# Three pieces of side work moved in a two-layer diffusion backbone on one core: modulation sums spread over a down projection, row scaling moved into a projection, output weights split later

## The chip, the cores and the metric

The kernel runs on one core of a Trainium2 chip. The metric is the device time in microseconds of one execution; the median of three runs is taken. The core's engines are TensorE (PE, with its weight loads PEld), VectorE (DVE), ScalarE (ACT), GpSimd (POOL) and SyncE (SP). All matrix work is done in float32 as three matmuls on split operands: every operand is written as a rounded high part (a cast on ACT) and a rest (a subtraction on DVE or POOL), and high×high, high×low and low×high are summed.

## The reference

Two layers over 1024 latent tokens and 256 context tokens of width 1024. Every layer computes a modulation of six rows from a condition vector, a mixer (attention), and a feed-forward block with a convolution along the sequence; each sub-layer ends in `LayerNorm(alpha*x + gate*f)`.

```python
m_lat = split(silu(c) @ ada_w[l] + ada_b[l], 6)          # shift, scale, gate, twice
h = x * (1 + m[1]) + m[0]
y = mixer(h)                                             # layer 0: global + neighbourhood; layer 1: window, sink
x = layer_norm(alpha * x + m[2] * y, ln_g[l, 0], ln_b[l, 0])
u = modulate(x, m[3], m[4]) @ w_up                       # 1024 -> 2 x 2816, three-tap convolution
f = (silu(g) * a) @ w_down                               # 2816 -> 1024
x = layer_norm(alpha * x + m[5] * f, ln_g[l, 1], ln_b[l, 1])
```

The modulation of a layer depends on nothing but `c` and `ada_w`, so it can be computed at any time before its use.

## The kernel before, in words

The kernel is a sequence of stages: the modulation of layer 0 and the first projections (to about 390 us of the trace), the two attentions of layer 0 (to about 807), their output projection, the feed-forward of the context (925 to 1130), that of the latent tokens (up 1130 to 1578, down 1578 to 1884), layer 1's projections (`l1_project`, 1884 to about 2025), its attention (`attn_c`, to 2279), its output projection (`l1_out`, to about 2384) and its feed-forward. Within most stages a scheduler orders the instructions of each engine; in the feed-forward (`ffn2`) and the attention the order is the order of the code.

**The down phase of `ffn2`.** The output of 1024 tokens by 1024 columns is made in two halves of 512 columns. A half has NP = 22 steps, one for each 128 rows of the hidden width; a step has eight token tiles of three matmuls (`mm`, lines 339 to 341), into eight PSUM banks. `load` (L1526 for weights of two steps, L1530 for the hidden rows `g`) fetches what a later step needs, six steps ahead (`last`), and splits it: ACT casts and DVE subtracts (L1536 and L1537 for g, L99 and L100 for weights). Steps 2 to 9 load a row tile z, steps 4 to 11 scale one (L1725, L1726). After the last step of the first half each bank is multiplied by the gate on DVE (`tt`, L1744), which frees the bank for the second half. The generator `side` computes layer 1's modulation ahead: `ada_ahead` has 24 pieces here; a piece loads 256 KB (L228, tile `araw`, two buffers) and, one piece later, DVE multiplies and adds twice (L235, L237). Every fourth piece's sum goes to DRAM (L241). SP issues all these loads in order, and one whose buffer is not free holds those behind it.

**`l1_project`.** `proj_tok` loads and splits weights (`load_in`, L112; cast L99, subtraction L100 on POOL), multiplies tile by tile, and hands each to `ev_q` (rotary on DVE, L381 and L391, and POOL, L395; then transposed, L416, and stored) or `ev_kv`. The order is: queries of the first 512 columns, context rows transposed (`build_hT`: four transposes L322, four evictions L328 into one `hst` buffer, then h and its rest, L333 and L334), keys and values, queries of the second 512 columns. The weights pass through `raw`, a pool of two buffers. `ada_reduce` sums the modulation's partial sums over partitions (load L271 into `accr`, cast L255, two small matmuls L259 and L260), two yields after each query tile.

**`attn_c` and `l1_out`.** `side` is a table of what runs beside which group of the attention: ten splits of output weights (`out_weight`, cast L1086, subtraction L1087), then sixteen row scalings (`scale_row`, L1892 and L1893 on POOL) of the rows x2 that `l1_out` reads. `l1_out` loads and splits the last three rows of weights before its first tile; for later tiles yh and yl are made of a loaded yr (L1141, L1142).

Of the kernel before, what the change touches and what calls it, by code (L numbers as in the profile page):

```python
# [17 lines left out]
KT = 8  # L18
# [18 lines left out]
class Kern:  # L37
# [229 lines left out]
    def ada_reduce(self, tp, bank, l, v, parts):  # L267
        for part in parts:
            for o in range(0, D, 512):
                acc = self.t(tp, [128, 512], "accr", bufs=2)  # L270
# [818 lines left out]

    def out_weight(self, w_out, k, h, r):  # L1090
# [23 lines left out]
    def out_project(self, w_out, yT, order, xsrc, gate_of, finish, st, wx, pp,  # L1114
# [6 lines left out]
        for k in range(5, KT):  # L1121
            r = self.t(self.raw, [128, 2, 512], "raw")
            nc.sync.dma_start(r, w_out[k * 128 : (k + 1) * 128].rearrange(
                "p (h n) -> p h n", n=512))
            for h in range(2):
                ws[k, h] = self.split_out(self.t(wx, [128, 2, 512], "w", R), r[:, h])
# [46 lines left out]
    def l0_out(self, h2l, h2c, pu):  # L1173
        nc, io, d = self.nc, self.io, self.d
        with ExitStack() as es:
# [5 lines left out]
            gates = {}  # L1181

# [303 lines left out]
    def ffn2(self, l, B, hps, T, dT, xsrc, gate_row, view, begin, finish, norm, jobs=(),  # L1486
# [209 lines left out]
        with ExitStack() as es, self.tc.manual_schedule(engines=every):  # L1696
# [20 lines left out]
            with ExitStack() as e2:  # L1717
# [13 lines left out]
                for i in range(NP):  # L1731
# [16 lines left out]
                    if 4 <= i < 4 + NLAT:  # L1748
                        scale(i - 4)
                    elif i > 4:  # L1750
                        for _ in range(3):
                            next(side, None)
                for _ in side:
                    pass
                bank = [self.t(pd, [128, 512], f"d{t}") for t in range(NLAT)]
                for i in range(NP, NP + 4):
                    load(i + last)
                    for t in range(NLAT):
                        mm(i, t, bank[t])
                    for t in (2 * (i - NP), 2 * (i - NP) + 1):  # L1760
                        add(0, t, tts[t])
            for i in range(NP + 4, 2 * NP - last):
# [22 lines left out]
    def l1_project(self, H, abc):  # L1785
        nc, io, d = self.nc, self.io, self.d
        with ExitStack() as es:
# [19 lines left out]

            def ev_kv(t, ps):
# [8 lines left out]
            def ev_q(h0):  # L1817
                def ev(t, ps):
                    q = self.t(st, [128, 512], "q", bufs=3)
                    self.rope(st, ps, 8, rp[:, t, 0:HD], rp[:, t, HD:], q)  # L1820
                    for _ in range(2):
                        next(sums, None)
                    return lambda: self.put_T(
# [14 lines left out]
            for t in range(2):  # L1838
                xc = self.t(st, [128, D], "xc", bufs=1)
# [27 lines left out]
    def attn_c(self):  # L1867
        nc, d, io = self.nc, self.d, self.io
        self.mix = (4, 10)
        with self.eC as es:  # L1870
# [8 lines left out]
            xp = es.enter_context(self.pool("cx"))  # L1879
            gb = [self.t(xp, [128, D], f"gb{i}") for i in range(2)]  # L1880
            self.bcast(gb[0], io["ln_g"][0, 1])
            self.bcast(gb[1], io["ln_b"][0, 1])

# [3 lines left out]
            def scale_row(t, h):  # L1887
                x = row()
                s = slice(h * 512, (h + 1) * 512)
                dr = d["x2"][t * 128 : (t + 1) * 128, s]  # L1890
                nc.sync.dma_start(x, dr)
                nc.gpsimd.tensor_mul(x, x, gb[0][:, s])  # L1892
                nc.gpsimd.tensor_add(x, x, gb[1][:, s])  # L1893
                nc.gpsimd.dma_start(dr, x)

            side = {}
            for i in range(10):
# [325 lines left out]
```

## Time and profile before

| | us |
|---|---|
| median of three runs (lowest, highest) | 3084.83 (3080.67, 3086.35) |
| profiled execution | 3084.81 |
| its span, first to last instruction | 3083.0 |
| PE busy | 2846.8 (92%) |
| DVE busy | 2087.5 (68%) |
| ACT busy | 1369.9 (44%) |
| POOL busy | 798.3 (26%) |
| mean granted clock of TensorE | 0.966 |

Busy time is an average over stages. A group of instructions has a line, an engine, an operation, its tiles (out<-in), a count, busy time and mean duration, then the idle time before it and what ended that. A row of a timeline has its start, its duration, and in brackets the idle time before it and what ended it. A row of SP is the issue of a DMA, not its transfer. A row of the windows has the length, then busy time and count for PE, PEld, DVE, ACT and POOL, the granted clock, the share of the DMA engines and GB/s.

### The profile page before, as it was taken

What the parts mean: (1) busy time and instruction counts of PE and PEld (TensorE: products, weight loads), DVE (VectorE), ACT (ScalarE), POOL (GpSimd) and SP (SyncE); (2) the same over time, 40 slices, a digit from 0 to 9 for tenths busy, and PEclk for the clock granted to TensorE, in tenths of its full rate; (3) what the DMA queues carried; (4) which work ended last, traced back from release to release, by engine and by line L of the source; (5) the groups of instructions that cost most, each with busy time, mean ns of one, the idle gap of its engine ahead of it and who ended that gap; (6) DMA issues with size and microseconds to landing.
All of it is one profiled execution on the core that took longest, in us unless ns stands there. A gap on an engine that the chain in (4) does not pass through costs nothing.

```text
span 3083.0 us, 44764 instructions
## 1 busy us (share of the span) xinstructions
PE 2846.8 (92%) x16564; PEld 2293.9 (74%) x16564; DVE 2087.5 (68%) x3705; ACT 1369.9 (44%) x2579; POOL 798.3 (26%) x961
## 2 busy tenths in 40 slices
PE   6889989899997989999999498989998899999998
PEld 2767767777787977888888476866677688888887
DVE  3687766666587877888876535356667677777755
ACT  2222155567435655444552234256653444545330
POOL 3651033354464420000000003336855000000001
PEclk7999999999998999999999799999999999999999
DMA  7366731023556544333365524443344322223742
GB/s 246 100 178 211 217 121 32 17 100 110 168 157 212 192 139 122 108 107 110 113 246 170 176 82 152 129 140 98 122 137 144 119 77 79 82 82 132 286 135 83
DMA packets 330039, 418.57 MB, mean 136 GB/s; under 512 B 22826, under 2 KB 245530, under 8 KB 328282
## 3 DMA queue, kind: packets, MB, share of 16 engines
q1 hardware_dynamic: 314124, 367.87, 38.1%
q0 software_dynamic: 12800, 46.14, 4.1%
q8 instruction: 130, 2.13, 0.3%
q10 hardware_dynamic: 2896, 1.70, 0.2%
q14 instruction: 89, 0.73, 0.1%
HBM read 318.85 MB, written 96.80 MB: 135 GB/s over the span
## 4 chain that ended last, share of the span: by engine, by line
PE 47%; DMA 4%; DVE 4%; POOL 4%; ACT 2%; issue 2%; SPq 0%; ACTq 0%; POOLq 0%; DVEq 0%
PE q L1546 8%; PE x L1546 8%; PE y L1546 8%; PE v L1546 4%; PE d L339 4%; PE d L341 4%; PE d L340 4%; PE mm L341 1%; PE mm L339 1%; PE mm L340 1%; POOL P L657 1%; PE pv L738 1%; DMA raw<-in_down_dram 1%; PE o L341 1%; PE T L729 1%
## 5 line engine op out<-in xcount | busy, mean ns | idle before, releaser
L657 POOL TENSOR_SCALAR P<-P,rin 128x640 f32<-128x640 f32 (+3 forms) x288 | 248.9, 869 | 311.1 <-DVE rin L656 281.3
L1448 DVE TENSOR_TENSOR w<-raw,w 128x512 fp32r<-128x512 f32 x308 | 208.8, 691 | 163.2 <-ACT w L1446 163.0
L339 PE MATMUL d<-w,w 128*128 128x512 f32 x704 | 276.1, 392 | 39.1 <-DVE tt L1744 39.1
L99 ACT CAST w<-raw 128x512 fp32r<-128x512 f32 x276 | 162.5, 620 | 256.7 <-PE d L341 126.2
L340 PE MATMUL d<-w,w 128*128 128x512 f32 x704 | 275.4, 391 | 0.0
L341 PE MATMUL d<-w,w 128*128 128x512 f32 x704 | 275.2, 391 | 0.0
L100 POOL TENSOR_TENSOR w<-raw,w 128x512 fp32r<-128x512 f32 x100 | 149.2, 1513 | 405.1 <-ACT w L99 403.7
L1593 POOL DMA_DIRECT2D g<-cv x44 | 23.5, 534 | 873.8 <-DVE cv L1592 873.8
L633 PE MATMUL S<-k,q 64*128 64x256 f32 (+2 forms) x1824 | 194.3, 339 | 15.7 <-DVE nm L1942 6.3
L100 DVE TENSOR_TENSOR w<-raw,w 128x512 fp32r<-128x512 f32 x176 | 135.4, 807 | 98.9 <-ACT w L99 98.8
L654 ACT ACTIVATE P<-P,nm 128x641 f32<-128x641 f32 (+4 forms) x208 | 161.6, 778 | 89.9 <-DVE nm L1942 33.8
L1446 ACT CAST w<-raw 128x512 fp32r<-128x512 f32 x308 | 182.5, 621 | 12.7 <-DVE raw L1453 11.4
L339 PEld LDWEIGHTS d<-w,w 128*128 128x128 f32 x704 | 133.2, 189 | 67.0 <-ACT w L99 39.5
L633 PEld LDWEIGHTS S<-k,q 64*128 64x128 f32 x1824 | 137.3, 189 | 51.8 <-issue 17.9
L644 ACT COPY PT<-T 128x512 f32<-128x512 f32 (+1 forms) x250 | 134.2, 566 | 84.1 <-PE T L764 79.8
L1537 DVE TENSOR_TENSOR w<-raw,w 128x512 fp32r<-128x512 f32 x176 | 112.5, 686 | 65.4 <-ACT w L1536 65.3
L340 PEld LDWEIGHTS d<-w,w 128*128 128x128 f32 x704 | 133.1, 189 | 27.7
L341 PEld LDWEIGHTS d<-w,w 128*128 128x128 f32 x704 | 133.0, 189 | 27.7
L778 PE MATMUL pv<-PT,v 128*64 128x128 f32 x2016 | 134.2, 281 | 14.6 <-ACT PT L644 12.0
L764 PE MATMUL T<-ident,P 128*128 128x128 f32 x1008 | 137.9, 284 | 9.5 <-POOL P L657 5.4
L1536 ACT CAST w<-raw 128x512 fp32r<-128x512 f32 x176 | 98.9, 618 | 106.1 <-PE d L341 56.4
L205 DVE SCALAR_TENSOR_TENSOR acc<-araw,cs,acc 128x512 f32<-128x512 f32 x168 | 132.0, 838 | 12.9 <-DMA araw<-in_ada_w_dram 12.4
(327 smaller groups left out, 7730.8 us busy)
## 6 DMA issues: line engine op xcount, KB each, us to landing
raw<-in_up_dram SPq DMA_DIRECT2D x132, 512.0 KB
raw<-g SPq DMA_DIRECT2D x88, 512.0 KB
raw<-in_down_dram SPq DMA_DIRECT2D x66, 512.0 KB
araw<-in_ada_w_dram SPq DMA_DIRECT2D x48, 512.0 KB
g<-cv POOLq DMA_DIRECT2D x44, 512.0 KB, 3.0
araw<-in_ada_w_dram SPq DMA_DIRECT2D x64, 256.0 KB
raw<-in_w_in_dram SPq DMA_DIRECT2D x28, 512.0 KB
wt<-in_ada_w_dram SPq DMA_DIRECT2D x16, 512.0 KB
```

Of the source, the lines that this page charges most:

```text
L99: nc.scalar.copy(hi, s)
L100: (lo_eng or nc.vector).tensor_sub(lo, s, f32(hi))
L339: nc.tensor.matmul(ps, lh, rh, start=first, stop=False)
L340: nc.tensor.matmul(ps, lh, rl, start=False, stop=False)
L341: nc.tensor.matmul(ps, ll, rh, start=False, stop=last)
L633: self.nc.tensor.matmul(outs[a], q[r, x, qs], k[r, y, ks], start=(i == 0), stop=(i == 2))
L654: nc.scalar.activation(P[:, :m], P[:, :m], AF.Exp, bias=negm, scale=-1.0, accum_out=den)
L657: nc.gpsimd.tensor_scalar(P[:, :n], P[:, :n], rin, 1.0, ALU.mult, ALU.mult)
L764: nc.tensor.transpose(ps[:, s * 128 : (s + 1) * 128], P[a][:, cols[i + x] : cols[i + x] + 128], self.ident,)
L1446: nc.scalar.copy(half(i, 0), src[i])
L1448: nc.vector.tensor_sub(half(i, 1), src[i], f32(half(i, 0)))
L1546: nc.tensor.matmul(ps, w[:, a, s], r[b][:, k], start=first and k + i == 0, stop=k == 3 and i == 2, skip_group_check=True,)
```

## The change

In the down phase a modulation piece is issued in each step from 1 to 21, also in those that scale a row, and one in each of the first four steps of the second half; before, three were issued in each of the steps 12 to 21. In `l1_project` each query tile scales one half row tile of x2 on DVE (`scale_rows`: load on SP, multiply, add, store on POOL's queue; two `xs` buffers), and the context rows use `raw` buffers; `accr` has one buffer where it had two. In `attn_c` the row scaling and its two broadcasts are gone, and four splits of output weights are left of ten; side[4] loads the rest. `l1_out` splits them before its first tile, into ten buffers where it had six.

```diff
@@ ada_reduce
-                acc = self.t(tp, [128, 512], "accr", bufs=2)
+                acc = self.t(tp, [128, 512], "accr", bufs=1)
@@ output weights
+    def load_out(self, pool, w_out, k):
+        r = self.t(pool, [128, 2, 512], "w" if pool is self.ring else "raw")
+        self.nc.sync.dma_start(
+            r, w_out[k * 128 : (k + 1) * 128].rearrange("p (h n) -> p h n", n=512)
+        )
+        return r
+
+    def out_rows(self, w_out, k0):
+        n = KT - 4
+        self.wrows = {
+            k: self.load_out(self.raw if k < n else self.ring, w_out, k)
+            for k in list(range(n, KT)) + list(range(k0, n))
+        }
@@ out_project
-        for k in range(5, KT):
-            r = self.t(self.raw, [128, 2, 512], "raw")
-            nc.sync.dma_start(r, w_out[k * 128 : (k + 1) * 128].rearrange(
-                "p (h n) -> p h n", n=512))
+        for k in range(KT):
+            if (k, 0) in ws:
+                continue
+            if k in self.wrows:
+                r = self.wrows[k]
+            else:
+                r = self.load_out(self.raw, w_out, k)
             for h in range(2):
-                ws[k, h] = self.split_out(self.t(wx, [128, 2, 512], "w", R), r[:, h])
+                w = self.t(wx if k < KT - 1 or not self.wrows else self.ring, [128, 2, 512], "w", R)
+                ws[k, h] = self.split_out(w, r[:, h])
@@ ffn2, down phase
                     if 4 <= i < 4 + NLAT:
                         scale(i - 4)
-                    elif i > 4:
-                        for _ in range(3):
-                            next(side, None)
-                for _ in side:
-                    pass
+                    if i:
+                        next(side, None)
                 bank = [self.t(pd, [128, 512], f"d{t}") for t in range(NLAT)]
                 for i in range(NP, NP + 4):
                     load(i + last)
                     for t in range(NLAT):
                         mm(i, t, bank[t])
+                    next(side, None)
                     for t in (2 * (i - NP), 2 * (i - NP) + 1):
                         add(0, t, tts[t])
+                for _ in side:
+                    pass
@@ l1_project
+            gb = {}
+
+            def scale_rows(i):
+                h, t = divmod(i, NLAT)
+                s = slice(h * 512, (h + 1) * 512)
+                if t == 0:
+                    for n in ("ln_g", "ln_b"):
+                        gb[n] = self.t(st, [128, 512], n)
+                        self.bcast(gb[n], io[n][0, 1, s])
+                x = self.t(st, [128, 512], "xs", bufs=2)
+                dr = d["x2"][t * 128 : (t + 1) * 128, s]
+                nc.sync.dma_start(x, dr)
+                nc.vector.tensor_mul(x, x, gb["ln_g"])
+                nc.vector.tensor_add(x, x, gb["ln_b"])
+                nc.gpsimd.dma_start(dr, x)
...
                     for _ in range(2):
                         next(sums, None)
+                    scale_rows(t + (NLAT if h0 else 0))
...
-                xc = self.t(st, [128, D], "xc", bufs=1)
+                xc = self.t(self.raw, [128, D], "raw")
@@ attn_c
-            for i in range(10):
-                side[2 + i] = lambda i=i: self.out_weight(io["w_out1"], i // 2, i % 2, row())
-            for i in range(16):
-                side[12 + i] = lambda i=i: scale_row(i // 2, i % 2)
+            side = {4: lambda: self.out_rows(io["w_out1"], 2)}
+            for i in range(4):
+                side[12 + 3 * i] = lambda i=i: self.out_weight(
+                    io["w_out1"], i // 2, i % 2, row()
+                )
@@ l1_out
-            wx = es.enter_context(self.pool("wx1", bufs=6))
+            wx = es.enter_context(self.pool("wx1", bufs=10))
```

On SP, in the down phase of layer 0 from the end of the scaling steps on, there stands before (`raw<-g` is the load of a step's hidden rows, `raw<-in_down_dram` that of two steps' weights, `araw` that of a modulation piece):

```order
L1530 DMA raw_16125<-g_96 128x1024
L228 DMA araw_16158<-in_ada_w_dram 128x2x256
L228 DMA araw_16160<-in_ada_w_dram 128x2x256
L228 DMA araw_16164<-in_ada_w_dram 128x2x256
L1530 DMA raw_16168<-g_96 128x1024
L228 DMA araw_16200<-in_ada_w_dram 128x2x256
L228 DMA araw_16205<-in_ada_w_dram 128x2x256
L228 DMA araw_16209<-in_ada_w_dram 128x2x256
```

And of the changed kernel, on the same queue at about the same steps (its line numbers are some 21 higher):

```order
L1551 DMA raw_16172<-g_96 128x1024
L228 DMA araw_16204<-in_ada_w_dram 128x2x256
L1551 DMA raw_16208<-g_96 128x1024
L228 DMA araw_16241<-in_ada_w_dram 128x2x256
L1547 DMA raw_16245<-in_down_dram 128x2x512
L1551 DMA raw_16253<-g_96 128x1024
L228 DMA araw_16285<-in_ada_w_dram 128x2x256
```

Between two loads of hidden rows stands one piece where three stood.

On TensorE, at the passage from the first query projection to keys and values in `l1_project`, there stands before (`tr<-ident,q` and `tr<-ident,xc` are transposes of a query tile and of context rows, `mm` 128x256 a matmul of the key and value projection):

```order
L416 MATMUL tr_18124<-ident_58,q_17997 128x128 x4
L416 MATMUL tr_18134<-ident_58,q_18051 128x128 x4
L339 MATMUL mm_18222<-w_18208,h1lh_17206 128x256
L340 MATMUL mm_18222<-w_18208,h1lh_17206 128x256
L341 MATMUL mm_18222<-w_18208,h1ll_17207 128x256
```

And of the changed kernel, on the same engine at the same place (the context rows are now named `raw`):

```order
L416 MATMUL tr_18168<-ident_58,q_18026 128x128 x4
L416 MATMUL tr_18178<-ident_58,q_18085 128x128 x4
L416 MATMUL tr_18188<-ident_58,q_18144 128x128 x4
L322 MATMUL tr_18200<-ident_58,raw_18198 128x128 x4
L322 MATMUL tr_18212<-ident_58,raw_18198 128x128 x4
L129 MATMUL small_18681<-ident_58,rt_18676 128x32
L322 MATMUL tr_18226<-ident_58,raw_18224 128x128 x4
L322 MATMUL tr_18238<-ident_58,raw_18224 128x128 x4
L339 MATMUL mm_18266<-w_18252,h1lh_17206 128x256
```

All transposes of the queries and of the context rows, and a small transpose of modulation rows, now stand ahead of the first matmul of keys and values. On SP the load of that matmul's weights stands behind stores of the transposed queries:

```order
L419 DMA qC_22_90<-qst_18173 128x4x128
L419 DMA qC_22_90<-qst_18183 128x4x128 x2
L112 DMA raw_18250<-in_w_in_dram 128x4x256
L265 DMA ada_88<-abr_18159 1x512
L419 DMA qC_22_90<-qst_18193 128x4x128 x2
L112 DMA raw_18258<-in_w_in_dram 128x4x256
```

Before, the same loads (`raw_18206` and `raw_18214`) stood among the stores of x2 at the end of the down phase.

More of the change, by code (lines that the diff above doesn't have):

```diff
@@ L1181, in l0_out @@
             gates = {}
+            self.wrows = {}
             def gate_of(t):
@@ L1878, in attn_c @@
             po = es.enter_context(self.pool("cO", bufs=1, space=PSUM))
[L1879 to L1882, printed above, removed]
             def row():
                 return self.t(Pp, [128, 641], "P")[:, :512]
[L1887 to L1896, printed above, removed]
-            for i in range(10):
-                side[2 + i] = lambda i=i: self.out_weight(io["w_out1"], i // 2, i % 2, row())
-            for i in range(16):
-                side[12 + i] = lambda i=i: scale_row(i // 2, i % 2)
+            side = {4: lambda: self.out_rows(io["w_out1"], 2)}
[3 more added lines that the diff above has]
+                )
             side[28] = lambda: self.out_y(d["yT1"], 0, [row(), row()])
```

## The prediction

> **What bounds the kernel now.** I read the page, then the waits of TensorE, then the windows and the timelines of the places that the diff touches. The page's first part:
>
> ```profile
> PE 2846.8 (92%) x16564; PEld 2293.9 (74%) x16564; DVE 2087.5 (68%) x3705; ACT 1369.9 (44%) x2579; POOL 798.3 (26%) x961
> ```
>
> TensorE is busy in 92% of the span, so 3083.0 − 2846.8 = 236 us is all that a change of order can recover. The longest of its waits (engine, tile, line, who it waited for; total, times, longest), and the rows of TensorE round it:
>
> ```profile
> PE d L339 <- DVE tt L1744: 39.1, 1, 39.1
> ```
>
> ```profile
> 1578.39 0.39 PE L339 MATMUL d<-w,w 128*128 128x512 f32 x1
> ...
> 1697.88 0.39 PE L341 MATMUL d<-w,w 128*128 128x512 f32 x1
> 1737.39 0.76 PE L339 MATMUL d<-w,w 128*128 128x512 f32 x1 [39.12 <-DVE tt L1744]
> ```
>
> These are the two halves of layer 0's down phase. The first half ran from 1578.39 to 1698.1 without a pause: 22 steps in 119.7 us, 5.44 us a step. Then TensorE stood 39.1 us, because its banks are free only when DVE has multiplied them (tt), and DVE was behind. The timeline of DVE shows by how much:
>
> ```profile
> 1645.19 1.22 DVE L1726 TENSOR_TENSOR z<-z,gb 128x1024 f32<-128x1024 f32 x1
> ...
> 1647.54 1.28 DVE L1537 TENSOR_TENSOR w<-raw,w 128x512 fp32r<-128x512 f32 x2
> ...
> 1709.39 2.04 DVE L237 SCALAR_TENSOR_TENSOR acc<-araw,cs,acc 128x256 f32<-128x256 f32 x4
> 1713.15 1.00 DVE L237 SCALAR_TENSOR_TENSOR acc<-araw,cs,acc 128x256 f32<-128x256 f32 x2 [1.72 <-DMA araw<-in_ada_w_dram]
> 1717.00 1.29 DVE L1537 TENSOR_TENSOR w<-raw,w 128x512 fp32r<-128x512 f32 x2 [2.84 <-ACT w L1536]
> ...
> 1735.35 1.29 DVE L1537 TENSOR_TENSOR w<-raw,w 128x512 fp32r<-128x512 f32 x2 [5.25 <-ACT w L1536]
> 1736.56 1.88 DVE L1744 TENSOR_TENSOR tt<-d,gate 128x512 f32<-128x512 f32 x3
> ```
>
> L1537 splits the g rows of one step. From the split at 1647.54 (step 12) to that at 1735.35 (step 21) nine steps took 87.8 us, 9.8 us each, and DVE idled in them. SP's timeline says why:
>
> ```profile
> 1628.35 21.66 SPq L228 DMA_DIRECT2D araw<-in_ada_w_dram  x3
> ...
> 1701.55 10.27 SPq L228 DMA_DIRECT2D araw<-in_ada_w_dram  x3
> 1711.88 0.46 SPq L1530 DMA_DIRECT2D raw<-g  x1
> ```
>
> Three modulation loads go out at a time, two buffers hold them, so the third waits for DVE, and the g load that DVE needs next stands behind it. Layer 1's down phase has the same steps without modulation, and there DVE's split ends just ahead of tt, with no wait of TensorE:
>
> ```profile
> 2947.71 2.50 DVE L1537 TENSOR_TENSOR w<-raw,w 128x512 fp32r<-128x512 f32 x4 [4.75 <-ACT w L1536]
> 2950.12 4.87 DVE L1744 TENSOR_TENSOR tt<-d,gate 128x512 f32<-128x512 f32 x8
> ```
>
> **Part 1, modulation one piece a step.** The work is the same 24 pieces. Each is two operations of 128x256; four of L237 took 2.04 us at 1709.39, so a piece is 1.0 us. Before step 12 eleven pieces are new: DVE ends step 11 at 1646.4 + 11.0 = 1657.4 at most, say 1659 with some waits for loads that are now more. TensorE needs the rows of step 17, which step 11 splits, at 1578.4 + 17 × 5.44 = 1671, so it isn't starved on the way. From there a step asks of DVE a g split of 1.3, half a weight split (0.65) and a piece (1.0), 2.9 us. SP couples them: the g load of a step now waits only for the piece of the step before last. From its issue at 1711.88 to the end of the split at 1718.3 it took 6.4 us; with a piece behind it that is 7.4 us. If two steps share such a round trip, a step is 3.7 us; if each pays a whole one, 7.4. I take 4.75, nearer the first, since one load may stay under way. DVE then reaches tt at 1659 + 9 × 4.75 + 2 = 1704, against TensorE's 1698.1: **a gap of about 5 us is left, −34** (0 at 3.7; at 7.4, 1659 + 67 + 2 = 1728, 30 left). The second half takes four more pieces; its rows are six steps ahead by then, so they cost nothing; without that lead they would cost 4.
>
> The gap has a tail, seen in windows (length, busy time of PE, PEld, DVE, ACT, POOL, granted clock, DMA share, GB/s):
>
> ```profile
> 1660.00:1698.00 38.00, 38.00 (x169) 31.36 (x167) 16.88 (x33) 6.86 (x12) 0.00 (x0) 1.00 0.51 166
> 1698.00:1737.00 39.00, 0.27 (x2) 0.00 (x0) 16.23 (x31) 7.45 (x13) 0.00 (x0) 0.55 0.53 173
> 1737.00:1745.00 8.00, 7.61 (x23) 6.06 (x24) 6.55 (x12) 1.67 (x3) 0.00 (x0) 0.65 0.64 255
> ```
>
> 23 matmuls took 7.61 us where the pace of the first row (38.00/169 = 0.225) asks 5.2: 2.4 us lost at a clock of 0.65. A short pause has a smaller tail. After the one of 6.33 us at 1884:
>
> ```profile
> 1884.27 1.97 PE L322 MATMUL d<-ident,z 128*128 128x128 f32 x8 [6.33 <-ACT z L2059]
> ...
> 1886.46 0.63 PE L340 MATMUL mm<-w,h1lh 128*128 128x512 f32 x1
> ...
> 1889.02 0.56 PE L340 MATMUL mm<-w,h1lh 128*128 128x512 f32 x1
> ```
>
> six matmuls from 1886.46 to 1889.02 went at 0.427, 1.2 us lost. I count half of the 2.4 as gained: **−1.2** (0 to −2.4). The Trainium skill ("TensorE: Matmul & The Clock Gate", What's actually happening) says that one idle window of some 3.4 us halves the clock, however long the pause was beyond that; by it a gap of 5 us keeps the whole tail, and the sum would be 1.2 us later. The row at 1884 lies between.
>
> **Part 2, ctx rows in the weights' buffers.** Both raw buffers now hold xc until its transposes, so the k/v weights load behind them. Now, the k/v splits and TensorE's two short waits at this place, with the chain's load of a weight:
>
> ```profile
> 1934.09 1.59 POOL L395 TENSOR_TENSOR q<-rp,rp 128x512 f32<-128x512 f32 x1 [4.80 <-PE mm L341]
> 1935.64 5.05 POOL L100 TENSOR_TENSOR w<-raw,w 128x512 fp32r<-128x512 f32 x4
> 1940.66 1.27 POOL L395 TENSOR_TENSOR q<-rp,rp 128x512 f32<-128x512 f32 x1
> ...
> 1948.33 1.28 POOL L334 TENSOR_TENSOR h1cl<-hst,h1ch 128x512 fp32r<-128x512 f32 x1 [0.36 <-DVE h1ch L333]
> ```
>
> ```profile
> 1941.99 0.66 PE L416 MATMUL tr<-ident,q 128*128 128x128 f32 x4 [0.72 <-POOL q L395]
> ...
> 1947.39 1.12 PE L322 MATMUL tr<-ident,xc 128*128 128x128 f32 x4 [2.18 <-ACT hst L328]
> ```
>
> ```profile
> 1940.72 4.04 DMA raw<-in_w_in_dram
> ```
>
> Count from the end of the q projection. The third q tile is transposed about 3.5 us later (rope, then L395), xc's first tile by 5.5. Its buffer is free then; the load takes 4.04, to 9.6. The cast on ACT now stands behind three evictions of xc, each held by the one hst buffer through a 1.28 us POOL subtraction, to about 12.5; POOL subtracts that eviction (1.28) and the weight (5.05/4 = 1.26), so full matmuls start at 15. The second half's weights are split by 20, while the first half's matmuls of four tiles fill TensorE. Idle is 15 less 4 of transposes, 11, where now 0.72 + 2.18 = 2.9 are: +8, and a clock tail of 1.2 to 2.4, +2: **+10**. Lower bound +3 (one load and cast barely uncovered, 4.04 + 0.62 + 1.26 − 2.9), upper +18 (the two loads and the evictions in series).
>
> **Part 3, row scaling in the q projections.** 32 DVE operations of 128x512, at 0.65 each (1.29/2, L1537), are 21 us over 16 tiles, 1.3 a tile where TensorE needs 8 × 3 × 0.23 = 5.5; hidden. The loads wait for stores two pieces back, and the modulation sums' loads queue behind those on SP, the more so with one accr buffer; the chain to TensorE's small matmuls has about one tile of slack. I take **+1** (0 to +8 if it stalls a little at each tile). A rule speaks against it: the Trainium skill ("GPSIMD Engine Reference", Specifications) says that GpSimd shares its memory port with DVE instructions that read two operands from SBUF, as these do; L395's 1.59 and 1.27 above, one operation with and without company, fit it. By it the last L395 may be 1.3 us later, and the sum 1.3 us higher, at the boundary only.
>
> **Part 4, what leaves the attention.**
>
> ```profile
> L1893 POOL TENSOR_TENSOR P<-P,gb 128x512 f32<-128x512 f32 x16 | 20.5, 1279 | 0.2
> L1892 POOL TENSOR_TENSOR P<-P,gb 128x512 f32<-128x512 f32 x16 | 20.4, 1278 | 2.3 <-DMA P<-x 2.3
> ```
>
> ```profile
> 2050.00:2110.00 60.00, 55.45 (x484) 38.54 (x480) 42.88 (x116) 43.38 (x102) 28.83 (x63) 1.00 0.28 85
> 2110.00:2230.00 120.00, 112.58 (x982) 75.98 (x980) 79.62 (x216) 81.39 (x187) 100.29 (x165) 1.00 0.37 115
> ...
> 2245.00:2260.00 15.00, 15.00 (x138) 10.54 (x136) 10.96 (x34) 12.21 (x30) 9.95 (x19) 1.00 0.06 19
> ```
>
> POOL loses 40.9 us, and 6 of 10 weight splits go. TensorE idled 4.6 us in the split stretch and 7.4 in the scaling stretch, and 0 where no side work ran: at most −12, and −2 of the start's two broadcasts. Most of the idle time in the attention is put down to ACT's copies, which the change does not touch:
>
> ```profile
> PE pv L738 <- ACT PT L644: 12.8, 23, 1.8
> ```
>
> I take half: **−6** (0 to −14).
>
> **Part 5, the first tile of the output projection.** Ten splits follow each other:
>
> ```profile
> L1086 ACT CAST w<-P 128x512 fp32r<-128x512 f32 x20 | 12.2, 621 | 9.1 <-DMA P<-in_w_out_dram 9.0
> L1087 DVE TENSOR_TENSOR w<-P,w 128x512 fp32r<-128x512 f32 x20 | 15.1, 770 | 9.8 <-ACT w L1086 9.8
> ```
>
> Each feeds three matmuls (0.69 us); four splits are ready ahead (2.7 us), so ACT at 0.62 keeps up and DVE at 0.65 to 0.77 loses at most 10 × 0.08. The second tile's yh cast then stands behind them and six up-weight casts: +3. Those casts and their DVE work no longer stand at the stage's end: −3. **0** (−3 to +4).
>
> **Sum** on the profiled execution (3084.81, span 3083.0 and 1.8 around it; the median is 3084.83): −34 − 1.2 + 10 + 1 − 6 + 0 = −30.2, **3054.6 us**.
>
> **Rivals.**
> - *The gap goes wholly and the attention recovers its idle time*: gap 0 and its tail (−41.5), kv +5, attention −12: 3036. For it: layer 1's tt; against: ACT named in the attention. 0.15.
> - *SP's coupling stays*: a whole round trip each step, 30 us left (−9), the rest as above (+5): 3081. For it: the 5.25 us wait before the last split; against: the third load, which made the wait, is gone. 0.1.
> - *Slower*: pieces in the scaling steps make DVE late from the start. If a step still costs what it did with three pieces, 9.8, in most of 21 steps (8.7 on the mean), the half takes 183 us where TensorE needs 119.7: 63 of waits instead of 39.1, +24, with +5 of the rest: 3114. It decides at (119.7 + 34)/21 = 7.3 us a step. Against: DVE's own work in a scaling step is 2.4 + 2.9 = 5.3. 0.05.
> - *Neither gap nor boundary moves much* (the gap half closed, −20, kv +18): 3084, no change. 0.05.
>
> **How the numbers follow.** Forecast 0.65, the rivals as given. A measurement tells apart about 0.2%, 6 us. Faster takes the forecast, the first rival and the near half of the second: 0.65 + 0.15 + 0.05 = 0.85; the other half and the last rival make 0.10 for the same; slower 0.05. The range reaches from 4 us under the first rival (its attention at −14, kv at +3) to the forecast with 13 us more of gap (half way to 7.4 a step) and kv at +18: 3032 to 3076. What it leaves out is the second rival's far half, the third, the last, and a little beyond the first.
>
> **What would show it.** Right: the wait on tt under 12 us; one araw between g loads on SP, steps of DVE under 5.44 us after 1660; a new wait of 5 to 15 us at the first k/v matmul, on w from POOL or ACT; no L1892 on POOL and TensorE busier in the attention. Wrong: a wait on tt above 20 us, waits inside the first half, or l1_project longer by over 20.

## The result, and the profile after

The changed kernel takes 3050.76 us (median of four runs, 3049.36 to 3058.9) beside 3082.75 for the kernel before: a ratio of 0.9903, interval 0.9879 to 0.9927, 32 us less. Forecast were 3054.6 and a range of 3032 to 3076. The profiled execution is the slowest of the four: span 3057.1, 25.9 less than before's 3083.0, where the sum said 30.2.

To see where the time went, each trace is cut at matmuls of TensorE: the first of layer 0's down phase, the first and last `mm` of layer 1's projection, the first and last score matmul S of its attention, the first and last matmul o of the output projection, and the first matmul v of the next feed-forward. The short passages between these stretches last as long as before (1.2 and 8.3 us).

| stretch (us) | before | after | difference | forecast |
|---|---|---|---|---|
| down phase and the transposes at its end | 307.5 | 272.6 | −34.9 | −35.2 |
| projection, first to last `mm` | 137.4 | 157.0 | +19.6 | +11 |
| attention, first to last S | 246.2 | 230.8 | −15.4 | −6 |
| output projection, first to last o | 94.4 | 100.1 | +5.7 | 0, with the next row |
| last o to the first v | 27.2 | 26.0 | −1.2 | |
| from there to the end | 682.4 | 682.3 | −0.1 | 0 |

The total was forecast well, but by two errors that cancel: the projection lost more, and the attention gained more. Each stretch is of one execution. Where an experiment below leaves the projection as changed, it takes 154.6 us (e2), 152.4 (e4) and 155.9 (e7) beside the 157.0 here, so differences of a few us in it mean little.

The down phase first. The waits of TensorE and its rows at the passage between the halves, after:

```profile
PE d L339 <- DVE tt L1765: 5.3, 1, 5.3
```

```profile
1698.33 0.39 PE L341 MATMUL d<-w,w 128*128 128x512 f32 x1
1703.97 0.76 PE L339 MATMUL d<-w,w 128*128 128x512 f32 x1 [5.26 <-DVE tt L1765]
```

The wait of 39.12 is one of 5.26. DVE and SP behind it, after:

```profile
1658.14 1.00 DVE L237 SCALAR_TENSOR_TENSOR acc<-araw,cs,acc 128x256 f32<-128x256 f32 x2
...
1661.54 1.29 DVE L1558 TENSOR_TENSOR w<-raw,w 128x512 fp32r<-128x512 f32 x2
...
1701.94 1.28 DVE L1558 TENSOR_TENSOR w<-raw,w 128x512 fp32r<-128x512 f32 x2
1703.15 4.87 DVE L1765 TENSOR_TENSOR tt<-d,gate 128x512 f32<-128x512 f32 x8
```

```profile
1667.02 0.37 SPq L228 DMA_DIRECT2D araw<-in_ada_w_dram  x1
...
1667.99 0.38 SPq L1551 DMA_DIRECT2D raw<-g  x1
1672.63 0.38 SPq L228 DMA_DIRECT2D araw<-in_ada_w_dram  x1
```

DVE ends step 11 at 1659.1 and splits step 12's rows at 1661.54 and step 21's at 1701.94: nine steps of 4.5 us, where they were of 9.8. SP still waits before a modulation load, but for 6.7 us at most in these steps (before the load at 1683.02), where rows of three loads stood for up to 21.66. Then the projection, as rows of TensorE and as a window (length, busy PE, PEld, DVE, ACT, POOL, clock, DMA share, GB/s):

```profile
1893.77 0.66 PE L259 MATMUL small<-ahl,ones 128*128 128x512 f32 x1 [2.56 <-DVE abr L264]
...
1910.79 0.63 PE L259 MATMUL small<-ahl,ones 128*128 128x512 f32 x1 [2.36 <-DVE abr L264]
...
1917.73 1.12 PE L322 MATMUL tr<-ident,raw 128*128 128x128 f32 x4 [1.60 <-ACT hst L328]
1920.08 2.12 PE L322 MATMUL tr<-ident,raw 128*128 128x128 f32 x8 [0.98 <-DVE m3s L287]
1924.92 1.22 PE L339 MATMUL mm<-w,h1lh 128*128 128x256 f32 x4 [2.73 <-ACT w L99]
1927.45 0.58 PE L340 MATMUL mm<-w,h1lh 128*128 128x256 f32 x1 [1.31 <-POOL w L100]
```

```profile
1911.00:1938.00 27.00, 18.58 (x95) 15.59 (x95) 14.60 (x28) 11.32 (x27) 16.07 (x15) 0.62 0.65 200
```

Before, the window at the same passage reads:

```profile
1941.00:1968.00 27.00, 23.96 (x189) 23.38 (x188) 8.10 (x30) 10.90 (x32) 13.81 (x15) 0.94 0.57 175
```

Of the six waits shown, the last two, on w, are those foreseen at the k/v weights; the one on `hst` was there before with 2.18 us, the one on `m3s` is new. The first two, on the bias row of the modulation sums, were not foreseen. In the 27 us of the window TensorE is busy for 18.58, where it was for 23.96, and the clock is at 0.62 for 0.94.

The text on the change says that each query tile scales one half row tile. So the code has it, but the scheduler moved the scaling forward. All sixteen pieces run on DVE between 1862.6 and 1954.6, the first nine beside the first query projection (its matmuls run from 1851.5 to 1908.0), the other seven at the passage and beside keys and values; the second query projection starts at 1962.2:

```profile
1952.60 0.69 DVE L1841 TENSOR_TENSOR xs<-xs,ln_g 128x512 f32<-128x512 f32 x1 [0.47 <-DMA xs<-x]
```

```profile
1962.22 0.47 PE L339 MATMUL mm<-w,h1lh 128*128 128x512 f32 x1
```

In the attention (between first and last S) the largest wait of before was `pv` on ACT's copies. Before, then after:

```profile
PE pv L738 <- ACT PT L644: 12.2, 22, 1.8
```

```profile
PE S L633 <- DVE nm L1966: 5.7, 3, 3.3
PE pv L738 <- ACT PT L644: 1.6, 5, 0.4
```

```profile
2095.00:2210.00 115.00, 113.14 (x998) 77.46 (x996) 82.13 (x222) 82.61 (x191) 57.95 (x127) 1.00 0.21 66
```

TensorE idles 1.9 us of 115 there, where it idled 7.4 of 120; ACT is busy for much the same share (72% and 68%), POOL for 50% where it was 84%.

And at the second tile of the output projection there are two new waits, on yh behind the splits and the up casts:

```profile
2261.59 0.50 PE L339 MATMUL o<-w,yh 128*128 128x512 f32 x1 [1.68 <-ACT yh L1161]
2263.29 0.80 PE L341 MATMUL o<-w,yl 128*128 128x512 f32 x1 [0.97 <-POOL yl L1162]
```

### The profile page after: what moved, and what is told of

It reads as the page before. It is cut to its first block, busy times and chain, and to the rows that moved or that the text cites. A ratio compares the mean times of both kernels' runs of the same rounds, so it can differ in the third digit from the quotient of the medians.

```text
span 3057.1 us, 44769 instructions
## 1 busy us (share of the span) xinstructions
PE 2857.3 (93%) x16564; PEld 2299.9 (75%) x16564; DVE 2110.7 (69%) x3737; ACT 1366.6 (45%) x2579; POOL 759.0 (25%) x929
## 3 DMA queue, kind: packets, MB, share of 16 engines
q1 hardware_dynamic: 313980, 367.87, 38.1%
## 4 chain that ended last, share of the span: by engine, by line
PE 49%; DMA 4%; DVE 4%; ACT 2%; issue 2%; POOL 1%; SPq 0%; ACTq 0%; POOLq 0%; DVEq 0%
PE q L1567 8%; PE x L1567 8%; PE y L1567 8%; PE v L1567 4%; PE d L339 3%; PE d L341 3%; PE d L340 3%; PE T L729 2%; PE pv L738 2%; PE S L633 2%; DMA raw<-g 1%; PE o L341 1%; PE o L339 1%; PE o L340 1%; PE mm L340 1%
## 5 line engine op out<-in xcount | busy, mean ns | idle before, releaser
L99 ACT CAST w<-raw 128x512 fp32r<-128x512 f32 x276 | 161.7, 620 | 256.7 <-PE d L341 98.9
L100 POOL TENSOR_TENSOR w<-raw,w 128x512 fp32r<-128x512 f32 x100 | 148.3, 1503 | 371.4 <-ACT w L99 370.0
L100 DVE TENSOR_TENSOR w<-raw,w 128x512 fp32r<-128x512 f32 x176 | 135.2, 805 | 100.8 <-ACT w L99 100.6
L1467 ACT CAST w<-raw 128x512 fp32r<-128x512 f32 x308 | 182.5, 620 | 8.5 <-DVE raw L1474 5.3
L778 PEld LDWEIGHTS pv<-PT,v 128*64 128x64 f32 x2016 | 110.4, 139 | 40.1 <-ACT PT L644 22.6
```

What stands on the lines that cost most here:

```text
L99: nc.scalar.copy(hi, s)
L100: (lo_eng or nc.vector).tensor_sub(lo, s, f32(hi))
L778: nc.tensor.matmul(O[a * HD : (a + 1) * HD], v_of(a, vts[i + x]), pT[:, s * 128 : (s + 1) * 128], start=(i + x == 0), stop=(i + x == m - 1 ...
L1467: nc.scalar.copy(half(i, 0), src[i])
```

## The experiments

Kernels of one group share runs of the kernel before on one chip: its median was 3082.56 in the first group (e1 to e4), 3086.85 in the second (e5 to e8) and 3086.86 in the third (e9 to e12). Between groups ratios to it are compared, not times. The stretches of the table above are given where they decide; each is of one profiled execution.

### e1: the spreading alone

In the kernel before, only this:

```diff
                     if 4 <= i < 4 + NLAT:
                         scale(i - 4)
-                    elif i > 4:
-                        for _ in range(3):
-                            next(side, None)
-                for _ in side:
-                    pass
+                    if i:
+                        next(side, None)
...
+                    next(side, None)
                     for t in (2 * (i - NP), 2 * (i - NP) + 1):
                         add(0, t, tts[t])
+                for _ in side:
+                    pass
```

> The kernel before with the modulation pieces spread, and nothing else. Theory (the down phase's wait was the third modulation load holding SP's queue, and the spreading by itself takes it away): the wait on tt falls from 39.1 to about 5 us, TensorE runs 34 to 36 us less from the start of the down phase to the start of the projection, the rest is unchanged: 3048 us beside 3083. Rival (part of the gain of the whole change comes from elsewhere, the spreading is worth less): over 3055.

Measured: 3047.56 us, ratio 0.9889 (0.9875 to 0.9902). The down stretch is 270.9, 36.6 shorter; the others are as before to 0.3 us. The waits of TensorE in its trace:

```profile
PE d L339 <- DVE tt L1744: 4.6, 1, 4.6
```

The theory holds. The spreading alone is worth as much as the whole change.

### e2: the spreading undone

The changed kernel with the removed lines of e1 put back and the added ones taken out.

> The changed kernel with three modulation pieces in each of steps 12 to 21 again; all other parts as changed. Theory (the parts add up; from the two traces the projections lose 19.6 us, the attention gains 15.4, the output projection loses 4.4): 8 to 9 us above the kernel before, 3091. Rival (the other parts lose nothing on most executions, the profiled one was a bad one, being 8 us above the three others): within 3 us of before, 3080 to 3086.

Measured: 3085.49 us, ratio 1.0006 (0.9997 to 1.0015), 2.9 us more than before at the medians; the wait on tt is back at 38.1. All other parts together are worth nothing that can be told. The time is the rival's, its reason only in small part: in this trace too the projection loses 17.2 us and the attention gains 15.8; the output projection and what follows it lose 1.6, where the changed kernel's profiled execution lost 4.5. Two large terms cancel.

### e3 and e4: the scaling, then the weights, back in the attention

e3 takes `scale_rows` out of the projection and puts `scale_row` and its broadcasts back:

```diff
-                    scale_rows(t + (NLAT if h0 else 0))
...
+            for i in range(16):
+                f = side.get(12 + i)
+                side[12 + i] = lambda i=i, f=f: (f and f(), scale_row(i // 2, i % 2))
```

> The changed kernel with the row scaling back in the attention on GpSimd, its broadcasts too; the output weights stay as changed. Theory (GpSimd's 41 us of scaling held the attention, and the xs loads hold SP's queue in the projection): the attention takes 8 to 10 us more, the projection 6 to 8 less, because the two waits of the small matmuls on the bias row (2.56 and 2.36 us) and their clock tails go: about 3052, against 3051. Rival (the output weights held the attention): the attention takes 2 us more or less, so 3044 to 3046.

Measured: 3056.53 us, ratio 0.9914 (0.9901 to 0.9928). The attention takes 243.4 instead of 230.8, the projection 144.9 instead of 157.0: +12.6 and −12.1. Both are larger than the theory had them, with its signs (the −12.1 is 7.5 against e4's 152.4 for the same code); the rival's 3044 to 3046 is out. The whole cannot be told from the changed kernel's 0.9903. In the attention the wait on ACT's copies is back:

```profile
PE pv L738 <- ACT PT L644: 9.7, 21, 1.1
```

ACT's work there was not touched by this edit: the row names the last link of a chain, and the scaling on POOL is what lengthened it. The likely way is through POOL's order, where the scaling stands ahead of the attention's own P: the wait of the transposes T on POOL's P grows from 0.8 to 4.0 us. The broadcasts and loads that came back with the scaling were not taken apart from it.

e4 leaves the scaling in the projection and puts ten weight splits back:

```diff
-            side = {4: lambda: self.out_rows(io["w_out1"], 2)}
-            for i in range(4):
-                side[12 + 3 * i] = lambda i=i: self.out_weight(
-                    io["w_out1"], i // 2, i % 2, row()
-                )
+            side = {}
+            self.wrows = {}
+            for i in range(10):
+                side[2 + i] = lambda i=i: self.out_weight(io["w_out1"], i // 2, i % 2, row())
...
-            wx = es.enter_context(self.pool("wx1", bufs=10))
+            wx = es.enter_context(self.pool("wx1", bufs=6))
```

> The changed kernel with ten splits of output weights in the attention's groups 2 to 11 again and three rows of weights at the output projection's start; the scaling stays in the projection. Theory (the scaling held the attention): the attention takes at most 4 us more, in its first third, and the output projection 4 to 5 less: 3049 to 3051. Rival (the splits held it): the attention takes 8 to 12 us more, 3055 to 3058.

Measured: 3057.31 us, ratio 0.9914 (0.9901 to 0.9928). The attention takes 237.0, +6.2, and the output projection 94.6, −5.5. The +6.2 lies between the two expectations (at most 4, and 8 to 12). So scaling and splits each held the attention, the scaling twice as much, and their sum, 18.8, is more than the 15.4 of both: they partly share the same waits. The wait on ACT's copies is 4.9 us in 7 waits here. The weights' part gains nothing that can be told, since the output projection gives most of its gain back.

### e5: two banks for the small matmuls

```diff
-            pa = es.enter_context(self.pool("pa1", bufs=1, space=PSUM))
+            pa = es.enter_context(self.pool("pa1", bufs=2, space=PSUM))
```

> The changed kernel with two PSUM banks for the modulation sums' small matmuls where it has one. Theory (SP, held at a load of x2 rows that waits for a store, issues the bias row late; DVE's addition then frees the one bank late, and TensorE waits 2.56 and 2.36 us for it): both waits and a good part of their clock tails go, 5 to 7 us less than the changed kernel, 3044 to 3046. Rival (the hold on SP reaches TensorE another way, by the load of the next sum): another wait of the small matmuls takes their place, within 2 us of 3051.

Measured: 3056.1 us, ratio 0.9894 (0.9878 to 0.9911), against 0.9903 for the changed kernel: no difference that can be told. The theory falls, the rival holds. The two waits are gone, and TensorE's waits in the projection now have this:

```profile
PE small L129 <- DVE abr L264: 5.1, 1, 5.1
...
PE tr L416 <- DVE m3s L287: 2.4, 1, 2.4
```

5.1 us for 4.9: the bank was not the cause. The changed kernel's trace shows a chain that leads there. POOL's store of a scaled piece, SP's next load with the bias row behind it, and DVE:

```profile
1899.11 0.56 POOL L1843 DMA_DIRECT2D x<-xs  x1 [2.77 <-DVE xs L1842]
```

```profile
1905.06 0.33 SPq L1840 DMA_DIRECT2D xs<-x  x1
...
1905.95 0.31 SPq L263 DMA_DIRECT2D abr<-in_ada_b_dram  x1
```

```profile
1908.16 0.69 DVE L1841 TENSOR_TENSOR xs<-xs,ln_g 128x512 f32<-128x512 f32 x1 [2.38 <-DMA xs<-x]
...
1909.97 0.67 DVE L264 TENSOR_TENSOR abr<-small,abr 1x512 f32<-1x512 f32 x1
1910.57 0.67 DVE L381 TENSOR_TENSOR rp<-mm,rp 128x512 f32<-128x512 f32 x1
```

SP held the load until 1905.06, 5.9 us after POOL issued the store of the piece whose buffer it needs (the sixteen stores of this trace landed 2.3 to 5.9 us after their issue). DVE stood 2.38 us for that load, with the bias row (L264) and the next tile's rotary (L381) behind it in order. By this reading, whichever of the two TensorE needs first gives the wait its name. In all, DVE waits 11.4 us for loads of these pieces, in seven waits.

### e6: key and value weights ahead of the context rows

```diff
+            wkv = self.load_in(w, 1024, 256, pool)
             for t in range(2):
                 xc = self.t(self.raw, [128, D], "raw")
...
-            self.proj_tok(pp, hT, lat + [8, 9], w, 1024, 256, ev_kv, pool)
+            self.proj_tok(pp, hT, lat + [8, 9], w, 1024, 256, ev_kv, pool, wkv)
```

(`proj_tok` takes split weights that are handed to it.)

> The changed kernel with the key and value weights taken into the two raw buffers ahead of the context rows. Theory (the weights' load and split behind the context rows' evictions is what TensorE waits for at the start of keys and values): the waits on w there (2.73, 1.31 and 0.71 us) and that on m3 and most of the clock of 0.62 in that stretch go; 7 to 9 us less, 3042 to 3044. Rival (the context rows now come too late): TensorE waits for them instead, at the same place or at the end of keys and values, within 3 us of 3051.

Measured: 3041.95 us, ratio 0.9858 (0.9837 to 0.9879). By ratio that is 14 us less than the changed kernel. The projection takes 146.3 instead of 157.0, 10.7 less (6 against e4's 152.4). The waits on w are gone, and the window at this passage reads:

```profile
1904.00:1931.00 27.00, 22.47 (x173) 21.58 (x172) 17.29 (x40) 11.29 (x31) 14.87 (x14) 0.94 0.62 182
```

The clock is 0.94 for 0.62, as before the change, and 173 matmuls go through for 95. The theory holds, with more than the 7 to 9 us that it said. The context rows come in time for the last tiles.

### e7: four pieces moved to the second half

```diff
-                    if i:
+                    if i and i not in (5, 7, 9, 11):
                         next(side, None)
...
-                    next(side, None)
+                    for _ in range(2):
+                        next(side, None)
```

> The changed kernel with the modulation pieces of steps 5, 7, 9 and 11 left to the second half, two in each of its first four steps. Theory (DVE's own work in the scaling steps makes the 5 us that are left on tt; each piece there is one microsecond): the wait on tt falls from 5.3 to 0 to 2 us with its clock tail, 4 to 7 us less, 3044 to 3047. Rival (the 5 us are SP's coupling in steps 12 to 21, not the scaling steps): the wait stays at 4 us or more, or the second half waits for DVE, within 2 us of 3051.

Measured: 3049.12 us, ratio 0.9874 (0.9856 to 0.9891). There is no wait on tt in this trace; the down stretch is 263.2 instead of 272.6, 9.4 less. Where the changed kernel crawled after its pause, this one does not:

```profile
1700.00:1712.00 12.00, 12.00 (x55) 9.93 (x54) 11.29 (x21) 2.62 (x5) 0.00 (x0) 1.00 0.48 146
```

By ratio the gain is 9 us, above the 4 to 7 of the theory, though the intervals overlap. The rival is out, and the theory has the place right: the pieces in the scaling steps made the 5 us that were left. But they were more than a microsecond of DVE each. From the start of the down phase to the split of step 12's rows DVE takes 72.1 us here for 82.7, 10.6 less; its busy time in it is 4.1 us less, the rest is time in which it waited, mostly for ACT's casts of weights (10.4 us, here 4.2). Whether it is the modulation loads, standing ahead of the weight loads on SP, that make those late was not tested.

### e8 and e9: the three edits together, twice

> The three edits together: two small banks, weights ahead of the context rows, four pieces moved to the second half. Theory (three separate places, each with its own wait): the gains add, 16 to 22 us less than the changed kernel, 3029 to 3035, and below the 3048 of the spread pieces alone. Rival (each pause's tail or the next wait takes some back): 3036 or more.

> The three edits together once more, as the kernel to compare with on the same chip as the next three. Both theories: its ratio to the kernel before as it was, 0.982 to 0.985, so 46 to 55 us less.

Measured: 3037.53 us, ratio 0.9835 (0.9819 to 0.9851), and in the third group 3032.43 us, ratio 0.9826 (0.9812 to 0.9839). Against 0.9903 that is 21 and 24 us less than the changed kernel (at 3086.9), the sum of e6 and e7. The theory's 16 to 22 holds by ratio; the times in the expectation count from a kernel before of 3083. The second small bank is not seen to add anything. The longest wait left in the projection stands at the start of keys and values, whose first matmul is at 1898.0, and is of the kind e5 showed; in e9:

```profile
1898.65 0.69 DVE L1842 TENSOR_TENSOR xs<-xs,ln_g 128x512 f32<-128x512 f32 x1 [3.60 <-DMA xs<-x]
...
1900.58 0.67 DVE L381 TENSOR_TENSOR rp<-mm,rp 128x512 f32<-128x512 f32 x1
```

```profile
1903.70 1.11 PE L416 MATMUL tr<-ident,q 128*128 128x128 f32 x4 [3.88 <-POOL q L395]
```

### e10: the store on another queue

```diff
-                nc.gpsimd.dma_start(dr, x)
+                nc.scalar.dma_start(dr, x)
```

> The three edits together, with the scaled rows stored by ACT's queue where GpSimd's stored them; nothing else. Theory (what is left in the first query projection is DVE standing in order behind a scaling whose load waits for the store two pieces back; a store takes about 5.9 us from GpSimd's issue to SP's next load, and that is the largest piece of the round trip): the round trip shortens, the wait of 5.1 us on q goes, 5 to 8 us less than the three edits. Rival (the round trip is the load and DVE's order, whoever stores; ACT's queue is held by its wait for DVE): within 3 us, or slower by ACT's later evictions.

Measured: 3034.04 us, ratio 0.9833 (0.982 to 0.9847), beside e9's 0.9826: no gain. The 3.88 us is gone, but the waits come back in small pieces, and the projection takes 143.3 beside 142.5. The waits on q were 7.7 us in four in e9; here the rows are:

```profile
PE tr L416 <- POOL q L395: 4.9, 5, 1.6
...
PE small L260 <- DVE ahl L256: 1.3, 1, 1.3
PE small L259 <- ACT ahl L255: 1.2, 3, 0.6
```

DVE's waits for loads of the scaled rows fall from 9.3 to 6.4 us, so the round trip is somewhat shorter, and nothing comes of it. The rival holds: who stores does not decide it. A third buffer for the scaled rows was not tried, so whether the round trip or DVE's added work is the larger share is left open.

### e11: half of the scaling in each place

```diff
-                    scale_rows(t + (NLAT if h0 else 0))
+                    if h0:
+                        scale_rows(t)
...
+            for i in range(8):
+                f = side.get(13 + 2 * i)
+                side[13 + 2 * i] = lambda i=i, f=f: (f and f(), scale_row(i, 1))
```

> The three edits together, with half of the row scaling (the first 512 columns) in the second query projection alone and the other half on GpSimd in the attention, in every second group. Theory (the harm in the projection comes from the first query projection, where the modulation sums share DVE and SP; the harm in the attention grows with the number of pieces): the projection loses its waits, 6 to 8 us less, the attention takes 4 to 6 us more: 0 to 4 us less in all. Rival (each place pays as soon as it has any scaling, by the broadcasts and the queue): the attention takes 10 us more, and the sum is slower than the three edits by 3 us or more.

Measured: 3037.08 us, ratio 0.9841 (0.9828 to 0.9855) beside 0.9826. The projection takes 136.9, no more than the 137.4 of before and 5.6 less than in e9, about what the theory said. The attention takes 237.4, 7.7 more, between the two expectations. The sum is 5 us worse at the medians, on the rival's side, but the intervals overlap.

The run does not show what the theory says of the place, though. The edit leaves the scaling in the code of the second query projection, and the scheduler moved it forward again: all eight pieces run beside the first, whose matmuls go from 1846.8 to 1899.1. The first two pieces and the last one:

```profile
1862.87 2.38 DVE L1842 TENSOR_TENSOR xs<-xs,ln_g 128x512 f32<-128x512 f32 x2
...
1899.00 0.69 DVE L1842 TENSOR_TENSOR xs<-xs,ln_g 128x512 f32<-128x512 f32 x1 [1.43 <-DMA xs<-x]
```

So eight pieces beside the first query projection, with all of its modulation sums there, cost nothing. In e9 the first eight cost nothing there either: its matmuls take 52.1 us from first to last, here 52.3, before 52.6. The loss of e9 is at keys and values, 41.2 us for 36.3 here and 36.4 before, beside which most of its second eight pieces run. Whether it is the round trip of loads and stores at this place that does the harm, the number of pieces in a row, or POOL's splitting of weights beside them (see below), is open. With one `accr` buffer in this run as in the changed kernel, that buffer alone is not what the projection lost by.

### e12: the kernel before with spreading and four pieces moved

> The kernel before with the pieces spread and four of them moved to the second half; nothing else of the change. Theory (parts add up; the rest of the change with its weights' order mended is worth 6 to 8 us): 0.9865, 6 to 8 us less than spreading alone and 4 to 10 us more than the three edits together. Rival (the rest of the change is worth nothing even mended): equal to the three edits within 3 us.

Measured: 3043.32 us, ratio 0.9863 (0.985 to 0.9877), 11 us more than e9 on the same chip, a little over the 4 to 10 of the theory; the rival is out. With the weights' order mended (and the second small bank), the other parts of the change are worth those 11 us: against this kernel e9's projection takes 142.5 for 137.5, its attention 229.7 for 248.4, its output projection 98.5 for 94.8. The best kernel of the study is e8 and e9's.

## Why the prediction was right, and where not

**The wait on tt, −34: right, by its own account.** DVE was to end step 11 at 1659 (1659.1), take 4.75 us a step (4.5), reach tt at 1704 (1703.15) and leave 5 us (5.26). The coupling through SP was there, but by the weights more than by the g rows: in these steps DVE waits 13.4 us for ACT's casts of weights (L99) and 2.4 for those of g. e1 shows the spreading alone does it, e7 that the rest came from the pieces in the scaling steps.

**The clock's tail, −1.2: wrong, no gain.** After 5.26 us of pause the window reads

```profile
1704.00:1712.00 8.00, 8.00 (x24) 6.38 (x25) 7.37 (x14) 2.28 (x4) 0.00 (x0) 0.65 0.67 195
```

24 matmuls at 0.225 are 5.4 us: 2.6 lost at a clock of 0.65, as the 2.4 at 0.65 after the 39.1 us. The failed step is "a short pause has a smaller tail", read from the pause of 6.33 us at 1884. That reading counted six matmuls and left out the eight transposes ahead of them: they took 1.97 us, where eight take 1.04 at 2023.51, and the clock of this window is like that of the other two:

```profile
1884.00:1892.00 8.00, 7.73 (x28) 6.52 (x29) 2.24 (x4) 3.12 (x9) 1.13 (x1) 0.66 0.72 218
```

The rule weighed there, of the Trainium skill ("TensorE: Matmul & The Clock Gate", What's actually happening), gave no gain; this trace agrees with it (0.65 after either pause). The tail is not the same each time, but its size does not follow the pause: in the 8 us from the end of e1's 4.62 us the clock is 0.79, after e2's 38.10 it is 0.77. e7, with no pause, has no tail. That the stretch as a whole gained 34.9, close to the 35.2 forecast, is chance: its second half ran 1 us shorter, within what it varies between traces.

**The k/v weights, +10: right.** e6 takes 10.7 us away by the order of the loads alone (6 against the shortest trace of the same code), and e3, which keeps the context rows in the weights' buffers and has no scaling, has a projection 7.5 us longer than before.

**The scaling in the projection, +1 (0 to 8): wrong in size, +5 to +12.** e3 is 12.1 us shorter without it; with the k/v weights mended, e6 is still 8.9 over before and e9 5.1. The failed step is "hidden", with "over 16 tiles" and "about one tile of slack". The sixteen pieces do not spread over both query projections: the scheduler runs them all before the second. And DVE's busy time was counted (1.3 us of a tile's 5.5) and the sums' chain on SP, but not that DVE, in order, stands for a load that waits for a store two pieces back, with the next tile's rotary behind it. e11 adds that half of the pieces cost nothing; why the other half does is open, as said there.

The other rule weighed there, of the Trainium skill ("GPSIMD Engine Reference", Specifications), that GpSimd shares its memory port with DVE instructions that read two operands from SBUF, was priced at the last L395 alone. That one is as long as before (1.26 us, 1.27 before). This case's rows fit the rule at another place, where POOL splits the k/v weights beside the scaling:

```profile
1931.14 1.76 DVE L1841 TENSOR_TENSOR xs<-xs,ln_g 128x512 f32<-128x512 f32 x1
1932.93 1.65 DVE L1842 TENSOR_TENSOR xs<-xs,ln_b 128x512 f32<-128x512 f32 x1
```

```profile
1930.63 3.40 POOL L100 TENSOR_TENSOR w<-raw,w 128x512 fp32r<-128x512 f32 x2
```

Most scaling operations take 0.69 us and these over 1.6; the 32 together take 26.3 us of DVE, where 21 were counted. POOL's L100 takes 1364 ns in the mean of the projection, and 1290 in e3, which has no scaling there. What share of the projection's loss this makes was not isolated by a run.

**The attention, −6 (0 to −14): wrong in size, −15.4.** The failed step is "put down to ACT's copies, which the change does not touch". e3 and e4 show those waits coming and going with POOL's scaling (9.7 us of them back) and with the splits on ACT and DVE (4.9). The idle time itself, −12 and −2 for the start, was the better guide.

**The output projection, 0 (−3 to +4): the size was off.** The second tile's yh costs what was said, about 3 us, with the waits of 1.68 and 0.97; what was to come back at the end, 3, is 1.2. Together +4.5 in this trace, and +1.6 in those of e2, e3 and e6. The difference is the clock behind the same two waits: in the 18 us from the first of them it is 0.81 here and 1.00 in those three.

**The sum.** −35 held; errors of +9 in the projection and −9 in the attention cancelled, which was luck, and the output projection's +4.5 is what the profiled execution lies above the sum. Of the rivals, the first named what the attention would do (its idle time recovered) with a gap of zero, which only the runs with e7's edit reached. The slower one did not come: DVE reached tt 124.3 us after the start of the down phase, 5.9 us a step over 21 steps, under the 7.3 at which it decides.

## What to carry to other kernels

Side work on an engine that runs in order is priced by what may stand behind its waits, not by its busy time: the same 24 pieces cost 39 us in threes and 5 one at a time, and 21 us of scaling that was to be hidden cost 5 to 12 in the projection, where DVE stood 11.4 us for loads of the pieces; half as many pieces cost nothing. Where a scheduler orders a stage, look in the trace for when side work runs: its place in the code told neither the prediction nor an experiment. Where TensorE waits for the last link of a chain, look for what stands in the queues of the links before it, and take the idle time of a stretch with no side work as the measure of what can be had. When a change's parts are moved together, run the one that carries the gain by itself: here it was worth all of it, and the rest only paid once the order of two loads was mended.

## What the runs showed of the hardware that was not expected

A pause of 5.26 us cost TensorE the same slow stretch as one of 39.12: 2.6 and 2.4 us lost over the next 8 us, both at a granted clock of 0.65; one of 38.10 (e2) cost as little as one of 4.62 (e1), with clocks of 0.77 and 0.79. The same two waits in the output projection, 2.4 to 2.7 us together, were followed by a clock of 0.81 over 18 us in the changed kernel, 0.91 in e5 and e9, and 1.00 in e2, e3 and e6. So a price of a pause read from one trace is good to some 3 us only. The stores of scaled rows, all of one size and issued by POOL, landed 2.3 to 5.9 us after their issue in one trace; the one issued at 1899.11 released the next load into its buffer 5.9 us later.
